# Layer 1's feed-forward output product: four of its eleven row blocks by seven half-size products, ordered by a build-time planner

## The chip, the cores and the metric

The kernel runs on one core of a Trainium2 chip. The metric is the device time of one execution in microseconds (us). The engines are PE (TensorE, the matrix multiplies; PEld is its weight load), DVE (VectorE), ACT (ScalarE), POOL (GpSimd) and SP (SyncE, which here only issues DMAs).

## The reference, cut to what matters

Two layers, each a mixer (a gated recurrence, then dilated attention) and a gated feed-forward part. There are 512 tokens, the model width is 1024, the inner width of the feed-forward part is 2816, and all is float32. The part that the change touches is the last product of layer 1:

```python
def swiglu_ffn(u, w_in, w_out):
    gate, up = jnp.split(u @ w_in, 2, axis=-1)
    return (jax.nn.silu(gate) * up) @ w_out        # (512 x 2816) @ (2816 x 1024)

y = swiglu_ffn(u, ffn_w_in[layer], ffn_w_out[layer])
h = h + (1.0 + g2) * rms_norm(y, norm_g[layer, 3])
```

`g2` is a row of 1024 numbers, the product of a conditioning vector with a 1024 x 1024 slice of `ada_w`, plus a bias.

## The kernel before

**How a float32 product is made.** Every operand is split into a high part, rounded to the fast float32 format by ACT (`act.copy`), and a low part, the rest, by DVE (`dve.tensor_sub`). A product is then three matmuls, high x high, high x low, low x high (`three`, L580). So each block of weights and each block of activations costs PE three passes, ACT one cast and DVE one subtraction. The views `SEEN`, `PLACED`, `SEEN2` and `PLACED2` (L38 to L41) bring every second element together, so a cast or a subtraction through them reads with a stride of two elements; `TAKE` and `LAID` do the same on PE's side.

**Weights.** `items` (L492 to L566) is the list of all loads in order, 1 MB each. `Stream` (L46) loads them through SP into two `raw` buffers; three pairs of `hi`/`lo` buffers hold split weights. Layer 1's list ends with 18 "quarters" items for the input product, then the 11 blocks of 256 rows of `w_out`, with the loads for `g2` (four "ada" items of 1 MB and two small "rows" items) woven in between.

**Layer 1's input product.** `seven_products` (L887) makes 18 column blocks by Strassen's scheme in Winograd's form: seven products of half size in place of eight. One pass per block: seven groups of twelve 256-column matmuls in the order `first`, `both`, `u2`, `first`, `u4`, `u2`, `u4`. ACT copies partial results from bank to bank between them (L993, L1002: `act.copy(s.u4, s.u2)`, on which the fifth group waits). The order on each engine is the order of the code (`manual_schedule`). At the end of a pass `gate_of` (L966, ACT) and `value_of` (L969, DVE) write one block of `mid`, the 2816 x 512 inner activations.

**Layer 1's output product** (`ffn`, L1060 to L1128). For j in 0 to 8: `st.take()` splits the weights of block j, two calls of `part` split two 128-row blocks of `mid`, and 48 matmuls of 512 columns (2 row blocks x 4 token blocks x 2 column halves x 3) add to eight PSUM banks, `y0` and `y1`. This loop lies in no hand-made order. The ada items are worked off inside `process_to` (L107): four DVE operations each (L397, L399), and per column half one all-reduce on POOL (L401) and two DVE operations on the gate (L446, L447). The last stage (L1107 to L1125) takes blocks 9 and 10 token block by token block, 24 matmuls each, then squares (L618), gates (L627), updates `h` and stores it.

**The planner** (`Plan`, L166; `planner`, L1471). The recurrence and the attention are laid out by it: each step is a task with an engine, a cost written by hand, the keys it reads and writes, and for PE a goal time. `run` computes due times backwards, tries 72 rules of a list schedule on those costs, and issues all tasks in the order of the best. `place` gives a ring of buffers; `load_next` issues the next load when a raw buffer comes free.

Of the kernel before, what the change touches and what calls it, by code (L numbers as in the profile page):

```python
# [17 lines left out]
P = 128  # L18
S = 512
# [298 lines left out]
def block_kernel(tc, x, c, positions, ada_w, ada_b, norm_g, hgrn_w_in, lower, hgrn_norm_g, hgrn_w_out,  # L318
# [8 lines left out]
    with ExitStack() as ctx:  # L327
# [237 lines left out]
        f1a, f1b = ffn_ws(1)  # L565
        items += f1a + weave(f1b[:9], ada_seq((1, 5)), 0) + f1b[9:]  # L566
        st = Stream(nc, wp, items, 2, 3)
# [318 lines left out]

        def seven_products(fs, mid, seeded, spare, th, tl):  # L887

# [80 lines left out]
            def value_of(i, s):  # L969
                dve.tensor_add(W[:, 3], W[:, 6 + i % 2], s.both)  # L970
                dve.tensor_add(W[:, 2], W[:, 4 + i % 2], s.u2)
                dve.scalar_tensor_tensor(H2(mid(fs[i])), W[:, 2:4], -1.0, W[:, 0:2], op0=OP.mult, op1=OP.mult)

            with tc.manual_schedule(engines=ORDERED):
# [10 lines left out]
                for i in range(len(fs)):  # L985
# [11 lines left out]
                    if before:  # L997
                        value_of(i - 1, before)
                    run(s.u2, Sm, 0, t2, False)
                    run(s.first, R, 1024, B21, False)  # L1000
                    act.copy(W[:, 4 + i % 2], s.both)
# [16 lines left out]
                gate_of(len(fs) - 1, before)  # L1018
                value_of(len(fs) - 1, before)

        def ffn(l, first, close, nxt, side):
            turns.close()
            close()
            with ExitStack() as fx:
# [4 lines left out]
                with ExitStack() as qx:  # L1029
# [6 lines left out]
                    for j in range(PLAIN[l]):  # L1036
# [14 lines left out]
                        if j == 0:  # L1051
                            cut()
                            fixed.close()
                    seven_products(range(2 * PLAIN[l], NF), mid, pss, spare, th, tl)
# [5 lines left out]
                y0 = [bank("mm") for _ in range(NT)]  # L1060
                y1 = [bank("a"), bank("b"), bank("a"), bank("b")]
                parts = {}

                def part(f):
                    oh, ol = fresh(roll, [P, S], "oh", 5, F32R), fresh(roll, [P, S], "ol", 5, F32R)
                    act.copy(PLACED(oh), SEEN(mid(f)))  # L1066
                    dve.tensor_sub(PLACED(ol), SEEN(mid(f)), PLACED(oh).bitcast(F32))
                    parts[f] = (oh, ol)
                NJ = NF // 2
                part(0)  # L1070
                part(1)

                def prods(t, f, w, k, halves=(0, 1)):
                    oh, ol = parts[f]
                    tok = slice(t * P, (t + 1) * P)
                    for n in halves:
                        a = slice(k * D + n * 512, k * D + (n + 1) * 512)
                        three((y0, y1)[n][t], oh[:, tok], ol[:, tok], w[0][:, a], w[1][:, a], f == 0, f == NF - 1)
                for j in range(NJ - 2):
                    if j == 2 and l == 0:  # L1080
                        with tc.tile_pool(name="angles", bufs=1, side=bass.opposite_side(side)) as rp:
                            rotary(rp)
                    w = st.take()
                    part(2 * j + 2)
                    part(2 * j + 3)
                    for k in range(2):
                        for t in range(NT):
                            prods(t, 2 * j + k, w, k)
                ws = [st.take(), st.take(1)]
                part(NF - 2)  # L1090
                part(NF - 1)
                mx.close()
                n = Turn(side, y0, y1, gates.pop((l, 5)), nxt and nxt[0])

# [375 lines left out]

        def planner(extra=(), end=0):  # L1471

# [26 lines left out]
            def load_next():  # L1499

                spot = seq[0] % (2 + len(extra))
                seq[0] += 1
                while st.items[to_load[0]][1] is None:
                    to_load[0] += 1
# [1012 lines left out]
```

## Time and profile before

| | |
|---|---|
| median of 3 runs | 1436.63 us (1436.47 to 1439.49) |
| profiled execution | 1437.54 us, its span 1435.7 us |
| PE busy, share of the span | 1406.7 us, 98% |
| DVE busy | 1119.5 us, 78% |
| ACT busy | 807.5 us, 56% |
| POOL busy | 204.9 us, 14% |
| mean granted TensorE clock | 0.997 of full speed |

The span runs from the first to the last instruction; what lies around it is 1.8 us. In the page a busy time is a sum over one engine's instructions, overlaps counted once; matmuls are pipelined, so a busy PE is one with no gap longer than its pipeline. Views by line give count, busy time, mean length of one in ns and the idle time before them with what ended it. The timeline gives start, length, engine, line, what is written and read, and the count of merged instructions.

### The profile page before, as it was taken

How to read it: one execution, taken by the hardware profiler on the slowest of the kernel's cores; microseconds unless marked ns; L12 is line 12 of the kernel's file. 1: busy time of each engine (PE TensorE's matmuls, PEld its weight loads, DVE VectorE, ACT ScalarE, POOL GpSimd, SP SyncE). 2: the span in 40 equal slices, each digit the busy share in tenths (PEclk: the TensorE clock that was granted, in tenths of full speed). 3: DMA queues.
4: the chain of work that ended last, by engine and by line, in shares of the span. 5: the costliest groups of instructions: out<-in, count | busy, mean ns of one | idle time of the engine just before them, and what ended most of it. 6: DMA issues, size and time to landing. Idle time of an engine off the chain costs nothing. (4 is left out here: it accounts for less than half of the span.)

```text
span 1435.7 us, 25151 instructions
## 1 busy us (share of the span) xinstructions
PE 1406.7 (98%) x9807; PEld 1304.7 (91%) x9807; DVE 1119.5 (78%) x1780; ACT 807.5 (56%) x1502; POOL 204.9 (14%) x179
## 2 busy tenths in 40 slices
PE   8999999999999999999999999999999999999998
PEld 6788899899999988888999999999988999999887
DVE  4589889587888898787888887888776978887644
ACT  4443434465655543376648888377876555555342
POOL 1023112130111112140001010001013111110100
PEclk9999999999999999999999999999999999999999
DMA  9655655132344377423254452444352434444541
GB/s 307 187 198 191 205 177 176 59 115 76 106 117 118 118 266 268 147 100 125 74 156 121 134 132 64 130 144 134 99 191 74 118 90 118 118 118 147 176 147 59
DMA packets 212871, 201.08 MB, mean 140 GB/s; under 512 B 8920, under 2 KB 170640, under 8 KB 212496
## 3 DMA queue, kind: packets, MB, share of 16 engines
q1 hardware_dynamic: 209776, 192.71, 43.0%
q10 hardware_dynamic: 1952, 6.65, 1.3%
q8 instruction: 77, 1.26, 0.4%
q0 software_dynamic: 1024, 0.12, 0.2%
q14 instruction: 42, 0.34, 0.1%
HBM read 192.30 MB, written 5.30 MB: 138 GB/s over the span
## 5 line engine op out<-in xcount | busy, mean ns | idle before, releaser
L1600 PE MATMUL ps_mm<-apart,hiq 128*128 128x256 f32 (+1 forms) x608 | 137.4, 320 | 1.6 <-ACT hiq L2113 0.8
L1600 PE MATMUL ps_mm<-uh,hiq 128*128 128x256 f32 (+1 forms) x416 | 134.6, 323 | 0.5 <-ACT ps_mm L2067 0.5
L1600 PE MATMUL ps_mm<-uh,loq 128*128 128x256 f32 (+1 forms) x416 | 131.2, 315 | 0.2 <-DVE loq L2025 0.2
L1600 PE MATMUL ps_mm<-ul,hiq 128*128 128x256 f32 (+1 forms) x416 | 131.0, 315 | 0.0
L1600 PEld LDWEIGHTS ps_mm<-apart,hiq 128*128 128x128 f32 x608 | 99.8, 191 | 7.7 <-ACT xs L2092 1.2
L954 DVE TENSOR_TENSOR loq<-raw,hiq 128x1024 fp32r<-128x1024 f32 x72 | 85.0, 1221 | 20.1 <-ACT hiq L950 20.1
L963 PE MATMUL ps_mm<-th,hiq 128*128 128x256 f32 x360 | 99.0, 275 | 0.0
L963 PE MATMUL ps_mm<-tl,hiq 128*128 128x256 f32 x360 | 99.0, 275 | 0.0
L963 PE MATMUL ps_mm<-th,loq 128*128 128x256 f32 x360 | 99.0, 275 | 0.0
L1600 PE MATMUL ps_mm<-apart,loq 128*128 128x256 f32 (+1 forms) x304 | 95.5, 314 | 0.7 <-DVE loq L2114 0.6
L934 POOL TENSOR_TENSOR raw<-raw 128x512 f32<-128x512 f32 x36 | 47.9, 1330 | 320.0 <-DVE spare L930 165.2
L1600 PEld LDWEIGHTS ps_mm<-uh,hiq 128*128 128x128 f32 x416 | 79.4, 191 | 5.1 <-ACT ps_mm L2067 0.9
L950 ACT CAST hiq<-raw 128x1024 fp32r<-128x1024 f32 x72 | 72.1, 1047 | 21.0 <-DVE raw L938 16.4
L1600 PEld LDWEIGHTS ps_mm<-uh,loq 128*128 128x128 f32 x416 | 79.4, 191 | 4.7 <-DVE loq L2025 0.4
L1600 PEld LDWEIGHTS ps_mm<-ul,hiq 128*128 128x128 f32 x416 | 79.4, 191 | 4.1 <-issue 0.5
L116 DVE TENSOR_TENSOR lo<-raw,hi 128x2048 fp32r<-128x2048 f32 x25 | 63.2, 2527 | 21.5 <-ACT hi L115 21.5
L1066 ACT CAST oh<-mid 128x512 fp32r<-128x512 f32 x44 | 37.4, 874 | 70.6 <-PE ps_b L583 61.9
L115 ACT CAST hi<-raw 128x2048 fp32r<-128x2048 f32 x25 | 47.6, 1905 | 43.0 <-DMA raw<-in_ffn_w_out_dram 31.6
L963 PEld LDWEIGHTS ps_mm<-th,loq 128*128 128x128 f32 x360 | 69.1, 192 | 0.0
L963 PEld LDWEIGHTS ps_mm<-tl,hiq 128*128 128x128 f32 x360 | 69.1, 192 | 0.0
L963 PEld LDWEIGHTS ps_mm<-th,hiq 128*128 128x128 f32 x360 | 69.1, 192 | 0.0
L582 PE MATMUL ps_mm<-hi,oh 128*128 128x512 f32 x176 | 66.9, 380 | 0.0
(475 smaller groups left out, 4800.7 us busy)
## 6 DMA issues: line engine op xcount, KB each, us to landing
raw<-in_ffn_w_in_dram SPq DMA_DIRECT2D x144, 256.0 KB, 4.0
raw<-in_ada_w_dram SPq DMA_DIRECT2D x32, 1024.0 KB, 6.2
raw<-in_ffn_w_out_dram SPq DMA_DIRECT2D x22, 1024.0 KB, 6.7
raw<-in_attn_w_in_dram SPq DMA_DIRECT2D x64, 256.0 KB, 4.4
raw<-in_attn_w_in_dram SPq DMA_DIRECT2D x12, 1024.0 KB, 5.2
raw<-in_hgrn_w_in_dram SPq DMA_DIRECT2D x11, 1024.0 KB, 5.4
third<-in_ada_w_dram SPq DMA_DIRECT2D x8, 1024.0 KB, 7.1
raw<-in_ffn_w_in_dram SPq DMA_DIRECT2D x8, 1024.0 KB, 6.3
```

Of the source, the lines that this page charges most:

```text
L115: self.nc.scalar.copy(hi, t)
L116: self.nc.vector.tensor_sub(lo, t, hi.bitcast(F32))
L582: pe.matmul(ps, ah, bh, start=start, stop=False, skip_group_check=part)
L934: pool.tensor_add(r[:, 2], r[:, 2], r[:, 0])
L950: act.copy(hi, src)
L954: dve.tensor_sub(lo, src, hi.bitcast(F32))
L963: pe.matmul(LAID(ps), w[x][:, a], TAKE(us[kt][y]), start=begin and kt + m == 0, stop=kt == 3 and m == 2, skip_group_check=True)
L1066: act.copy(PLACED(oh), SEEN(mid(f)))
L1600: pe.matmul(LAID(dst()), x, TAKE(y), start=begin and i == 0, stop=i == len(todo) - 1, skip_group_check=True)
```

## The change

Layer 1's output product is rebuilt. Its row blocks 0 to 3 (1024 of 2816 rows) are taken by seven products of half size, two token halves by two column halves by the even and odd 128-row blocks. Each product has 24 matmuls of 512 columns, in four steps j of six. For this their weights come as four "quarter" items (even or odd rows by column half, 1 MB each) in place of four row blocks. The sums of quarters are formed in place by DVE (`b_sub`), the sums of `mid` blocks too (`a_op`), and every sum is split again (`b_cut`, `a_cut`). Blocks 4 and 5 stay plain products, as pieces that the planner can put between; blocks 6 to 8 follow, and blocks 9 and 10 are split in the plan and multiplied in the old last stage. Seven more raw buffers are opened where `seven_products` had its scratch. All four engines' work of this stage, SP's loads included, is issued in the planner's order. The first product's operands are split earlier, in the last pass of `seven_products` (`OutStart`, called between its groups `u2` and `first`): one cast and one subtraction of 1024 strided elements and four of 512. Layer 0 is unchanged.

The products and plain pieces are named by the pairs of PSUM banks they add to (`F`, `U`, `E`, `Z`). The first seven-product step begins with `behind_first`, which also puts two matmuls into `U`.

```diff
-        items += f1a + weave(f1b[:9], ada_seq((1, 5)), 0) + f1b[9:]
+        SEVEN = 4
+        def quarter_items():
+            v = ffn_w_out[1].rearrange("(j k p) (n c) -> p k n j c", k=2, p=P, n=2)
+            return [("w", v[:, q // 2, q % 2, 0:4], None) for q in range(4)]
...
+        last_gate = ada_seq((1, 5))
+        items += f1a + quarter_items() + f1b[SEVEN:SEVEN + 2] + last_gate[0] + f1b[SEVEN + 2:SEVEN + 3] + last_gate[1] + last_gate[2]
+        items += f1b[SEVEN + 3:9] + last_gate[3] + last_gate[5] + f1b[9:]
...
                     run(s.u2, Sm, 0, t2, False)
+                    if sooner and not more:
+                        sooner()
                     run(s.first, R, 1024, B21, False)
...
+        class OutStart:
...
+            def __call__(self):
+                self.ring = st.part_tiles(0)
+                (hi, lo), src = self.a_place(0), groups_of(self.midt, 0, 0, 0)
+                act.copy(PLACED2(hi), SEEN2(src))
+                dve.tensor_sub(PLACED2(lo), SEEN2(src), PLACED2(hi).bitcast(F32))
+                for k in range(4):
+                    raw = st.raw[st.done][:, k * 512:k * 512 + 512]
+                    act.copy(uh[:, k], raw)
+                    dve.tensor_sub(ul[:, k], raw, uh[:, k].bitcast(F32))
...
+            extra = [roll.tile([P, 2048], F32, name=f"rawx{k}") for k in range(SEVEN)]
...
+            cost = lambda g, c: c * (0.08 + 0.23 * size(g))
+            def b_place():
+                def make():
+                    b_no[0] += 1
+                    k = (b_no[0] - 1) % 4
+                    return uh[:, k], ul[:, k]
+                return plan.place("B", 4, make)
...
+            def b_cut(j, q, ready=False):
+                b = b_place()
+                key = key_at(q, j)
+                if not ready:
+                    ACT(0.52, lambda: act.copy(b.t[0], at(q, j)[0]), [key], [b("h")])
+                    DVE(0.62, lambda: dve.tensor_sub(b.t[1], at(q, j)[0], b.t[0].bitcast(F32)), [key, b("h")], [b("l")])
+                return b
...
+            def b_sub(j, to, one, two):
+                DVE(0.61, lambda: dve.tensor_sub(at(to, j)[0], at(one, j)[0], at(two, j)[0]), [key_at(one, j), key_at(two, j)], [key_at(to, j)])
...
+            def a_cut(t, k, g, src=None, key=None, ready=False):
+                a = a_next()
+                if not ready:
+                    src = groups_of(midt, t, k, g) if src is None else src
+                    key = ("mid", 2 * t + k, g) if key is None else key
+                    ACT(cost(g, 1.0), lambda: act.copy(PLACED2(a.t[0]), SEEN2(src)), [key, ring()], [a("h")])
+                    DVE(cost(g, 1.15), lambda: dve.tensor_sub(PLACED2(a.t[1]), SEEN2(src), PLACED2(a.t[0]).bitcast(F32)), [key, a("h")], [a("l")])
+                return a
...
+            def a_op(g, f, to, one, two):
+                DVE(cost(g, 1.15), lambda: f(to[0], one[0], two[0]), [one[1], two[1]], [to[1]])
...
+            def product(dst, cut, q, begin, behind=None, ready=0):
+                for j in range(SEVEN):
+                    if j in (0, 4):
+                        a = cut(j // 4)
+                    b = b_cut(j, q, j < ready)
...
+                    PE(6 * 0.2159, go, [a("h"), a("l"), b("h"), b("l"), ring()], [d() for d in dst])
...
+            def behind_first(j):
+                b_sub(j, 0, 1, 0)
+                if j == 1:
+                    PE(0.43, lambda: [pe.matmul(U[t].t, uh[:, 0, 0:P], uh[:, 0], start=True, stop=True) for t in range(2)], [], [U[t]() for t in range(2)])
+            product(F, lambda g: a_cut(0, 0, g, ready=g == 0), 0, True, behind_first, 4)
+            for t in range(2):
+                ACT(0.5, lambda t=t: act.copy(U[t].t, F[t].t), [F[t]()], [U[t]()], urgent=True)
...
+            def first_sum(g):
+                a_op(g, dve.tensor_add, s1, a21, a22)
+                return a_cut(0, 0, g, *s1)
...
+            product(E, first_sum, 0, True, lambda j: b_sub(j, 0, 3, 0))
...
+            plain_splits(SEVEN)
+            plain_products(SEVEN, "FZ", True)
+            product(F, lambda g: a_cut(0, 1, g), 2, False)
+            plain_splits(SEVEN + 1)
+            plain_products(SEVEN + 1, "FZ")
+            product(U, second_sum, 0, False, lambda j: b_sub(j, 0, 2, 0))
+            for t in range(2):
+                DVE(0.61, lambda t=t: dve.tensor_add(E[t].t, U[t].t, held.t[:, t * 512:t * 512 + 512]), [U[t](), held(t)], [E[t]()], urgent=True)
+            product(Z, lambda g: a_cut(1, 1, g), 0, False, lambda j: b_sub(j, 1, 3, 1))
+            plain_products(SEVEN, "E")
+            product(E, fourth_sum, 3, False)
+            product(U, third_sum, 1, False)
+            plain_products(SEVEN + 1, "E")
...
+            for j in (SEVEN, SEVEN + 1):
+                plain_products(j, "U")
+            for j in range(SEVEN + 2, NF // 2):
+                plain_splits(j)
+                if j < NF // 2 - 2:
+                    plain_products(j)
...
+                n = 2 + len(extra)
+                spot = seq[0] if seq[0] < n else held + (seq[0] - n) % (n - held)
```

## Rows read from the trace of the kernel before

**Rows 1.** Page: span and busy time, share of the span and instructions, of each engine.

```profile
span 1435.7 us, 25151 instructions
PE 1406.7 (98%) x9807; PEld 1304.7 (91%) x9807; DVE 1119.5 (78%) x1780; ACT 807.5 (56%) x1502; POOL 204.9 (14%) x179
```

**Rows 2.** Busy time of each engine by stretch; columns in the first line.

```profile
core 0: us, PE busy (x) PEld busy (x) DVE busy (x) ACT busy (x) POOL busy (x), PEclk, DMA share, GB/s
1315.80:1408.50 92.70, 92.70 (x432) 81.16 (x431) 54.02 (x51) 35.44 (x31) 6.87 (x2) 1.00 0.44 148
```

**Rows 3.** ACT's timeline, last stage: the squares that follow each finished PSUM bank.

```profile
1419.33 0.60 ACT L618 ACTIVATE junk<-ps_b 128x512 bf16<-128x512 f32 x1
1424.51 0.60 ACT L618 ACTIVATE junk<-ps_a 128x512 bf16<-128x512 f32 x1
```

**Rows 4.** DVE by line and form, 1303 to 1412 us.

```profile
L116 DVE TENSOR_TENSOR lo<-raw,hi 128x2048 fp32r<-128x2048 f32 x11 | 27.0, 2453 | 12.8 <-ACT hi L115 12.8
L1067 DVE TENSOR_TENSOR ol<-mid,oh 128x512 fp32r<-128x512 f32 x22 | 18.1, 834 | 13.4 <-ACT oh L1066 13.4
L399 DVE SCALAR_TENSOR_TENSOR shared<-raw,cond,shared 128x512 f32<-128x512 f32 x14 | 10.5, 749 | 4.8 <-DMA raw<-in_ada_w_dram 4.6
```

**Rows 5.** ACT by line and form, same stretch.

```profile
L115 ACT CAST hi<-raw 128x2048 fp32r<-128x2048 f32 x11 | 21.0, 1907 | 29.5 <-DMA raw<-in_ffn_w_out_dram 27.8 <-PE ps_mm L963 1.8
L1066 ACT CAST oh<-mid 128x512 fp32r<-128x512 f32 x22 | 18.5, 868 | 26.0 <-PE ps_b L583 21.7 <-PE ps_mm L583 3.7 <-PE ps_mm L963 0.6
```

**Rows 6.** ACT and DVE by line and form in the planned attention stage, 650 to 1090 us.

```profile
L2049 ACT CAST hiq<-raw 128x1024 fp32r<-128x1024 f32 x32 | 33.5, 1046 | 9.0 <-DVE raw L2029 7.7 <-PE ps_mm L1600 0.9 <-DMA raw<-in_attn_w_in_dram 0.2
L2024 ACT CAST hiq<-raw 128x512 fp32r<-128x512 f32 x48 | 29.6, 616 | 21.6 <-DVE raw L2029 14.3 <-DMA raw<-in_attn_w_in_dram 6.9
...
L2029 DVE TENSOR_TENSOR raw<-raw 128x512 f32<-128x512 f32 x64 | 43.7, 688 | 4.4 <-DMA raw<-in_attn_w_in_dram 3.4
```

**Rows 7.** DVE's timeline, attention: a run of equal instructions (start, length, xcount).

```profile
694.94 4.62 DVE L2160 TENSOR_TENSOR loq<-raw,hiq 128x1024 fp32r<-128x1024 f32 x4
```

**Rows 8.** ACT's timeline, last pass of layer 1's input products.

```profile
1308.24 0.38 ACT L993 COPY ps_mm<-ps_b 128x256 f32<-128x256 f32 x1
```

**Rows 9.** Chain that ended last: the products of that pass (start, length, xcount).

```profile
1308.91 1.36 PE ps_mm L963 x12
1311.61 4.02 PE ps_mm L963 x36
```

**Rows 10.** ACT's and DVE's timeline: last silu, last mid block, runs of strided and plain work.

```profile
1319.79 0.41 ACT L967 ACTIVATE shared<-ps_mm 128x256 f32<-128x256 f32 x1
...
1316.68 2.33 DVE L1067 TENSOR_TENSOR ol<-mid,oh 128x512 fp32r<-128x512 f32 x3
...
1322.54 0.68 DVE L972 SCALAR_TENSOR_TENSOR mid<-shared 128x512 f32<-128x512 f32 x1
```

**Rows 11.** DVE and POOL side by side: one subtraction under an all-reduce.

```profile
1329.48 4.07 DVE L116 TENSOR_TENSOR lo<-raw,hi 128x2048 fp32r<-128x2048 f32 x1 [0.17 <-ACT hi L115]
...
1328.78 3.64 POOL L401 PARTITION_ALL_REDUCE shared<-shared  x1 [28.67 <-DVE shared L399]
```

**Rows 12.** Busy time by stretch in planned stages (columns as in rows 2).

```profile
690.00:710.00 20.00, 20.00 (x182) 20.00 (x181) 18.55 (x31) 11.04 (x18) 1.65 (x2) 1.00 0.35 113
910.00:930.00 20.00, 18.39 (x159) 17.75 (x158) 18.37 (x21) 8.70 (x9) 0.00 (x0) 1.00 0.33 98
...
650.00:1090.00 440.00, 431.67 (x3192) 408.17 (x3191) 349.58 (x756) 310.60 (x661) 35.64 (x38) 1.00 0.43 125
60.00:260.00 200.00, 197.85 (x1228) 175.87 (x1227) 175.92 (x288) 86.04 (x190) 40.90 (x32) 1.00 0.55 184
```

**Rows 13.** What PE waited for in the planned attention stage: us, times, longest.

```profile
PE ps_mm L1600 <- DVE loq L2160: 2.1, 4, 0.6
```

**Rows 14.** Page, DMA issues: the layers' output weights, KB each, us to landing.

```profile
raw<-in_ffn_w_out_dram SPq DMA_DIRECT2D x22, 1024.0 KB, 6.7
```

**Rows 15.** A stretch in which the granted clock fell (columns as in rows 2).

```profile
10.00:20.00 10.00, 6.93 (x43) 5.63 (x44) 7.12 (x17) 7.27 (x15) 2.89 (x4) 0.83 1.10 343
```

More of the change, by code (lines that the diff above doesn't have):

```diff
@@ L885, in token_sums, with seven_products @@
             return cut
-        def seven_products(fs, mid, seeded, spare, th, tl):
+        def seven_products(fs, mid, seeded, spare, th, tl, sooner=None):
             fs = list(fs)
@@ L1019, in seven_products, with groups_of, __init__, a_place @@
                 value_of(len(fs) - 1, before)
+        def groups_of(midt, t, k, g):
+            j = slice(0, min(4, SEVEN)) if g == 0 else slice(4, SEVEN)
+            return midt[:, 2 * j.start + k:2 * j.stop + k - 1:2, t * 256:t * 256 + 256]
+        class OutStart:
+            def __init__(self, midt):
+                self.midt = midt
+            def a_place(self, g):
+                return [t[:, g * 1024:g * 1024 + 1024].rearrange("p (s c) -> p s c", c=256) for t in self.ring]
+            def __call__(self):
[7 more added lines that the diff above has]
+                    dve.tensor_sub(ul[:, k], raw, uh[:, k].bitcast(F32))
@@ L1053, in ffn @@
                             fixed.close()
-                    seven_products(range(2 * PLAIN[l], NF), mid, pss, spare, th, tl)
+                    sooner = None if nxt else OutStart(midt)
+                    seven_products(range(2 * PLAIN[l], NF), mid, pss, spare, th, tl, sooner)
                 fl.drain()
@@ L1059, in ffn @@
                     st.fill()
-                y0 = [bank("mm") for _ in range(NT)]
-                y1 = [bank("a"), bank("b"), bank("a"), bank("b")]
+                NJ = NF // 2
                 parts = {}
[L1064 to L1071, printed above, removed]
                 def prods(t, f, w, k, halves=(0, 1)):
@@ L1077, in prods @@
                         a = slice(k * D + n * 512, k * D + (n + 1) * 512)
[L1078 to L1088, printed above, removed]
@@ L1089, in ffn, with part @@
-                ws = [st.take(), st.take(1)]
-                part(NF - 2)
-                part(NF - 1)
+                        three((y0, y1)[n][t], oh[:, tok], ol[:, tok], w[0][:, a], w[1][:, a], f == 0, f == NF - 1, nxt is None)
+                if nxt is None:
+                    y0, y1, ws = out_planned(midt, sooner, roll, parts)
+                else:
+                    y0 = [bank("mm") for _ in range(NT)]
+                    y1 = [bank("a"), bank("b"), bank("a"), bank("b")]
+                    def part(f):
+                        oh, ol = fresh(roll, [P, S], "oh", 5, F32R), fresh(roll, [P, S], "ol", 5, F32R)
+                        act.copy(PLACED(oh), SEEN(mid(f)))
+                        dve.tensor_sub(PLACED(ol), SEEN(mid(f)), PLACED(oh).bitcast(F32))
+                        parts[f] = (oh, ol)
+                    part(0)
+                    part(1)
+                    for j in range(NJ - 2):
+                        if j == 2 and l == 0:
+                            with tc.tile_pool(name="angles", bufs=1, side=bass.opposite_side(side)) as rp:
+                                rotary(rp)
+                        w = st.take()
+                        part(2 * j + 2)
+                        part(2 * j + 3)
+                        for k in range(2):
+                            for t in range(NT):
+                                prods(t, 2 * j + k, w, k)
+                    ws = [st.take(), st.take(1)]
+                    part(NF - 2)
+                    part(NF - 1)
@@ L1092, in ffn @@
                 mx.close()
-                n = Turn(side, y0, y1, gates.pop((l, 5)), nxt and nxt[0])
+                n = Turn(side, y0, y1, gates.pop((l, 5)) if nxt else gates.pop((l, 5)).t, nxt and nxt[0])
                 def mm(t, ks=range(4)):
@@ L1468, in block_kernel, with planner @@
         pre.close()
-        def planner(extra=(), end=0):
+        def planner(extra=(), end=0, held=0):
             plan = Plan()
@@ L1499, in load_next @@
             def load_next():
-                spot = seq[0] % (2 + len(extra))
+                n = 2 + len(extra)
+                spot = seq[0] if seq[0] < n else held + (seq[0] - n) % (n - held)
                 seq[0] += 1
+                if to_load[0] == len(st.items):
+                    return
                 while st.items[to_load[0]][1] is None:
```

91 lines of the change are left out of this document (added).

## The prediction

> **What bounds the kernel now.** I read the page first: PE is busy for 1406.7 of 1435.7 us, 98% of the span, DVE for 78% [rows 1]. So the time is PE's work plus the little that PE waits. Then the stage that is changed, by stretches: from 1315.8 to 1408.5 us PE is busy for all 92.7 us with 432 matmuls, at a granted clock of 1.00, while DVE is busy for 54.0 and ACT for 35.4 [rows 2]. That is nine blocks of 48 matmuls and no wait at all. A matmul removed here is therefore time gained in full, and a wait of PE that is new here is time lost in full; DVE has 38 us to spare on the whole, and the question is whether that spare lies where the change wants it.
>
> **Saved on PE.** In the last stage the second squares of two successive token blocks start at 1419.33 and 1424.51 [rows 3], 24 matmuls apart: 5.18 / 24 = 0.216 us for a matmul of 512 columns. Four plain blocks are 4 x 48 = 192 matmuls, seven half-size products 7 x 24 = 168. Minus 24 matmuls is -5.18 us; the two that open bank U are +0.43. **Sum -4.75 us.** What is planned is then 408 matmuls and those two, 88.5 us, where 93.3 stood.
>
> **The earlier start (OutStart).** It is put into the last input pass, on ACT between the copy to `u2` and the copy to `u4`, on which PE's fifth group waits. ACT begins it behind the copy of 1308.24 [rows 8]. That copy was held up by a cast of 2048 elements, which leaves this place; PE's first group ends at 1307.57 by the chain (1308.91 - 1.34 [rows 9]), so the copy of 0.38 is done at 1307.9. One strided cast of 1024: a plain 512 takes 616 ns and a plain 1024 takes 1046 [rows 6], a strided 512 takes 868 [rows 5]; so 1046 + 2 x (868 - 616) = 1550, some 1.5 in a row of casts. Four plain casts of 512 at 0.52 in a row (half of 1046) are 2.1. ACT is free at 1311.5, then come two copies, 0.28 and 0.36: `u4` is ready at 1312.1. PE wants it at 1311.6 by the chain [rows 9], at 1311.3 if a pipeline's length is taken off. **A wait of 0.6 us** (0.45 to 0.75) on a step that had none. DVE's part, one strided subtraction and four plain, ends by 1313.4 and is covered by PE's last two groups, which without it would wait for nothing.
>
> **The second product's start.** In the old code nobody waited for the last block of `mid`. Now DVE's order has `value_of` ahead of all planned work: it waits for PE's last group, ACT's silu (0.41) and its own 0.68 [rows 10], so DVE is free about 1.35 us after PE has begun the first product. Then a sum of 1024 (1.2), ACT's strided cast (1.5), DVE's strided subtraction (1.45), one plain low part (0.6) and three hand-overs of 0.15 (0.17 stands in [rows 11]): 6.5, or 7.1 if one more subtraction is put between. PE ends the first product and the two matmuls after 5.6. **A wait of 0.9 to 1.5 us.**
>
> **DVE's load in the seven products.** In a row, 1024 plain elements take 4.62 / 4 = 1.155 us [rows 7]; 512 plain 0.69 alone [rows 6] and about 0.61 in a row; 512 strided 2.33 / 3 = 0.77 [rows 10]; 1024 strided 1.155 + 2 x (0.834 - 0.69) = 1.44 [rows 4]. Up to the last step of the last product: 6 strided low parts of `mid` 8.6, 4 sums of them 4.6, 16 sums of quarters 9.8, 24 low parts of quarters 14.6, weights and `mid` parts of blocks 4 and 5 4.6 + 3.1, two adds 1.3. That is 46.6 us. DVE at its densest is busy for 18.55 and 18.37 of 20 us in the planned attention [rows 12], 92%: 46.6 / 0.92 + 1.35 = 52.0. PE needs the last step after six products and U's opening (31.5), the first halves of blocks 4 and 5 (10.4), one quarter of block 4 (2.6) and three steps (3.9): 48.4, or 51.0 if the planner brings the quarter of block 5 forward. So PE waits for 1.0 to 3.6 us in this half, the start of the second product among them. I take the middle of 1.0 and 3.6, and never less than the start: **2.4 us**. Rings of four B and two A places keep DVE from working further ahead.
>
> **The rest of the stage.** Blocks 6 to 10 need 5 x (2 x 1.155 + 2 x 0.77) = 19.3 us of DVE, the last adds 2.6, the gate 16 sums of 0.69 (0.749 alone [rows 4], less in a row) and four of 0.65, 13.6. DVE's whole is 82.1. One subtraction of 2048 took 4.07 us under POOL's all-reduce [rows 11], where the other ten took (27.0 - 4.07) / 10 = 2.29 [rows 4]; one such hit adds 1.8. 83.9 / 0.92 + 1.35 = 92.5, due some 3 us after PE's 88.5 (block 10's second half and the second gate are wanted 2.6 and 5.2 us into the last stage): 1.0 us of wait, less than the 2.4 that PE has waited by then, so it costs nothing more. ACT has under 50 us of work here and is covered. The planner's own costs count strided work as plain (1.15 and 0.62 for DVE, 1.0 and 0.52 for ACT), so its order comes true later than it reckons; that is in the above, which goes by rows.
>
> **Loads.** 1 MB lands in 6.7 us in the median [rows 14]. The two first quarters load during the input passes as blocks 0 and 1 did. The third can start once the scratch of the last but one pass is free, the next behind the sixth group of the last pass, 1.3 us ahead of the stage. At the 343 GB/s of [rows 15] 1 MB takes 3.1 us; at 3.6 each, overlapped, block 4 lands at 7 and block 5 at 11, ahead of their use at 16 and 21. Cost 0; one by one at 6.7 it would be 18.8 and 25.5, the bound that a rival takes.
>
> **Sum.** -4.75 + 0.6 + 2.4 = -1.75 us. Against the profiled execution, 1437.54 us (span 1435.7 and 1.8 around it), that is 1435.8; the median of the runs lies 0.9 lower, at 1436.63, so 1434.9.
>
> **A page against a row.** A strided cast of 512 takes 868 ns where a plain one takes 616 [rows 5, 6], and a strided subtraction 834 [rows 4] where a plain one takes 688 [rows 6].
> The Trainium skill, page SBUF — State Buffer, section Door 1, says that a compute engine may stride up to four float32 elements at full bandwidth, as long as accesses fall twice into a 16-byte line; a stride of two should then cost nothing. By it the load of the first half would fall to 44.3 and the sum would come to about -3.3. The rows here speak against it, and the sum stays with them.
>
> **Rivals.**
> *Waits absorbed.* The planner finds an order in which DVE runs ahead on the plain pieces of blocks 4 and 5, and PE waits only for OutStart and 0.5 more: -3.65, 1433.0 us. For it: from 690 to 710 us PE has no gap beside a DVE at 18.55 of 20 [rows 12], and the longest of PE's waits for a low part in attention is 0.6 [rows 13]. Against it: the late start of DVE by 1.35.
> *DVE becomes the bound.* Both all-reduces hit it (82.1 + 3.6 = 85.7) and it is busy for 88% only, as in the planned recurrence, 175.9 of 200 [rows 12]: 97.4 + 1.35 - 3 = 95.7 for PE's 88.5, a wait of 7.2: +3.05, 1439.7 us, **slower**. It decides where DVE's share in the stage falls below 85.7 / 94.3 = 91%. For it: attention's mean is 349.6 of 440, 79%, with PE waiting for 8.3. Against it: that DVE idled there for want of work too.
> *OutStart holds PE's reads.* It writes the first half of the tiles `uh` and `ul` while PE reads their second half. If those reads wait for the writes, the fourth group starts at 1313.4 and not at 1310.3: +2.5 more, 1437.4 us.
> *Loads one by one.* Block 4's weights are late by 3.6 in part beside the same wait: +2.5, 1437.4 us.
> *The clock.* From 10 to 20 us PE is busy for 6.9 of 10 and the granted clock is 0.83, between its levels of 1.2 and 2.4 GHz [rows 15]; in the planned stages, with PE's waits in them, it is 1.00 [rows 12]. If a product of 24 matmuls ran at the lower level: +5.2, 1440.1 us.
> The Trainium skill, page TensorE: Matmul & The Clock Gate, section What's actually happening, has an idle array lose half its pulses.
>
> **Chances.** Within 0.2% means 2.9 us either way, about what a measurement of this kernel tells from no change. Forecast 0.41 (its own range 1433.4 to 1436.2; 0.08 of it beyond the bound), waits absorbed 0.26, DVE the bound 0.17, held reads 0.08, late loads 0.06, clock 0.02. Faster 0.26 + 0.08 = 0.34; slower 0.17 + 0.02 = 0.19; same 0.47. The range goes from no wait at all, 1431.9, to the DVE-bound case, 1439.7, which leaves out the upper half of that case, the clock and little below.
>
> **What would show it.** In the changed profile the stage has 410 matmuls to the last stage; PE's waits list a low part or a sum (DVE) two or three times, together 1.5 to 3 us, most within 50 us of the stage's start; the copy to `u4` of the last pass starts at 0.6 us after its group could. Wrong would be: waits of PE in that list above 5 us or below 1, a wait for a DMA, a fourth group that waits for OutStart, or a clock below 1.00.

## The result: slower by 0.45%, and the profile after

The changed kernel takes 1444.79 us (median of nine runs, 1440.18 to 1448.25) beside 1438.15 us for the kernel before on the same chip. **The ratio is 1.0045, 95% interval [1.0028, 1.0063]: some 6.5 us slower.** The forecast was 1434.9 us, in a range that ended at 1439.7; the measured time lies beyond it. The kernel before came out 1.5 us higher too, at 1438.15 where the forecast started from 1436.63, so change stands against change: +6.6 for -1.75.

**Where the two traces part.** Up to the last input pass of layer 1 both kernels run the same work in the same order, but that pass begins anywhere from 1304 to 1315 us in the profiles of this study, without the change having a hand in it. Whole spans therefore say little about one profile. What follows compares the *last stretch*: from the first matmul of the last input pass to the end of the span. In the kernel before the pass starts at 1306.23 us by the chain, so the stretch is 1435.7 - 1306.23 = 129.47 us. In the changed kernel it starts at 1308.90: 1443.8 - 1308.90 = 134.90 us. **The change costs 5.4 us there**, which lies within the interval of the ratio (4.0 to 9.1 us).

The page of the changed kernel, answering to [rows 1]:

```profile
span 1443.8 us, 25203 instructions
PE 1406.6 (97%) x9785; PEld 1302.8 (90%) x9785; DVE 1148.2 (80%) x1836; ACT 823.6 (57%) x1538; POOL 207.1 (14%) x179
```

There are 22 matmuls fewer, 24 removed and two added, as planned. PE is yet no less busy, and 8 us more of the span are idle (1443.8 - 1406.6 = 37.2, where it was 29.0). The waits of PE in the last stretch (us in total, times, longest) say where:

```profile
PE ps_b L1178 <- ACT uh L1098: 4.4, 1, 4.4
PE ps_a L595 <- DVE loq L1152: 1.6, 2, 0.8
PE ps_a L594 <- ACT hiq L1151: 1.1, 1, 1.1
```

The same stretch by windows (columns as in [rows 2]):

```profile
1314.00:1324.00 10.00, 6.87 (x51) 6.36 (x49) 4.95 (x8) 3.23 (x8) 0.00 (x0) 1.00 0.33 107
1324.00:1331.00 7.00, 5.70 (x18) 4.69 (x19) 5.73 (x9) 4.47 (x8) 0.00 (x0) 0.76 1.05 408
...
1331.00:1391.00 60.00, 60.00 (x279) 52.54 (x278) 59.47 (x77) 37.64 (x49) 3.25 (x1) 1.00 0.28 93
```

PE loses time at both ends of the stage: the first two rows show the start, and the waits at L594 and L595 above lie in the last stage. In the 60 us of the third row it waits for nothing, though DVE is busy for 59.47 of 60 (in [rows 2] it was 54.0 of 92.7).

**The first loss: the two matmuls that open bank U.** They stand at L1178, in the middle of the first product. The chain in order of time (start, length, what):

```profile
1321.24 0.29 ACT shared L979
...
1321.56 0.70 DVE mid L984
...
1322.28 1.24 DVE shared L1119
...
1323.60 1.13 ACT hiq L1112
1324.72 0.53 ACT uh L1098
...
1325.30 0.73 PE ps_b L1178 x2
1326.03 4.28 PE ps_a L1131 x12
```

The two matmuls only have to open the bank; their operand is any tile, and the code takes `uh[:, 0]`, without naming it among the keys that the task reads. `uh[:, 0]` is the first of four B places. The plan, which knows of no reader, issues the cast for the second product's first step into that place (L1098) ahead of them. They then wait for that cast. On ACT it stands behind the cast of the second product's A operand (L1112), and this waits for the sum (L1119), the last block of `mid` (L984) and silu (L979). So the whole chain that the prediction reckoned for the *second* product's start has come to stand in the middle of the *first*: 4.43 us of wait. The 12 matmuls behind it take 4.28 us where 24 take 5.18, and the granted clock of that window is 0.76. Together (0.73 - 0.43) + (4.28 - 2.59) = 2.0 us more.

**The second loss: the last loads.** The end of the chain:

```profile
1399.00 5.11 DMA rawx<-in_ada_w_dram
...
1407.36 3.24 POOL shared L1776
...
1411.35 0.70 DVE gate L1806
1412.07 2.06 DMA rawx<-in_ffn_w_out_dram
...
1417.09 1.05 ACT hiq L1151
...
1418.17 1.24 DVE loq L1152
...
1419.45 0.48 PE ps_a L595
1419.93 0.22 PE ps_a L596
```

Each load starts where a DVE instruction has freed its buffer, down to the load of block 10, which waits for the last gate row to be read (L1806). The last stage's first token block has three matmuls that wait, 2.7 us in total, and loses 3.7 us with what the restarts cost (four of its matmuls take 0.48, one in a row 0.22).

One thing ahead of the prediction has to be put right here. It says that seven more raw buffers are opened. The code opens four (`range(SEVEN)`, with `SEVEN = 4`). Four of the six buffers hold the quarters for most of the stage, and only two are left to take turns.

**The sum.** 6.4 us at the opening, 3.7 at the end, less the 4.75 of saved matmuls: +5.4 us, the measured 134.90 - 129.47.

**What came as reckoned.** DVE's operations by line and form, as in [rows 4] and [rows 7]:

```profile
L1152 DVE TENSOR_TENSOR loq<-rawx,hiq 128x1024 fp32r<-128x1024 f32 x10 | 12.0, 1224 | 3.1 <-ACT hiq L1151 3.1
...
L1113 DVE TENSOR_TENSOR loq<-mid,hiq 128x1024 fp32r<-128x1024 f32 x4 | 6.2, 1559 | 0.2 <-ACT hiq L1112 0.2
L1113 DVE TENSOR_TENSOR loq<-shared,hiq 128x1024 fp32r<-128x1024 f32 x2 | 2.8, 1410 | 0.0
```

A strided subtraction of 1024 takes 1410 to 1559 ns (reckoned: 1.44 us) where a plain one takes 1224. The Trainium skill, page SBUF — State Buffer, section Door 1, has a stride of two float32 elements cost nothing; these rows, like [rows 4, 6], do not agree.

### The profile page after: what moved, and what is told of

The parts are those of the page before. It is cut to its first block, busy times and chain, and to the rows that moved or that the text cites. A ratio compares the mean times of both kernels' runs of the same rounds, so it can differ in the third digit from the quotient of the medians.

```text
span 1443.8 us, 25203 instructions
## 1 busy us (share of the span) xinstructions
PE 1406.6 (97%) x9785; PEld 1302.8 (90%) x9785; DVE 1148.2 (80%) x1836; ACT 823.6 (57%) x1538; POOL 207.1 (14%) x179
## 3 DMA queue, kind: packets, MB, share of 16 engines
q0 software_dynamic: 1024, 0.12, 0.2%
## 5 line engine op out<-in xcount | busy, mean ns | idle before, releaser
L975 PE MATMUL ps_mm<-th,hiq 128*128 128x256 f32 x360 | 99.0, 275 | 0.0
L975 PE MATMUL ps_mm<-tl,hiq 128*128 128x256 f32 x360 | 99.0, 275 | 0.0
L975 PE MATMUL ps_mm<-th,loq 128*128 128x256 f32 x360 | 99.0, 275 | 0.0
L946 POOL TENSOR_TENSOR raw<-raw 128x512 f32<-128x512 f32 x36 | 48.0, 1334 | 319.8 <-DVE spare L942 165.1
L975 PEld LDWEIGHTS ps_mm<-tl,hiq 128*128 128x128 f32 x360 | 69.1, 192 | 0.0
L975 PEld LDWEIGHTS ps_mm<-th,hiq 128*128 128x128 f32 x360 | 69.1, 192 | 0.0
L975 PEld LDWEIGHTS ps_mm<-th,loq 128*128 128x128 f32 x360 | 69.1, 192 | 0.0
L1826 PEld LDWEIGHTS ps_mm<-apart,loq 128*128 128x128 f32 x304 | 58.3, 192 | 4.7 <-DVE loq L2340 1.0
L595 PE MATMUL ps_mm<-ul,hi 128*128 128x256 f32 (+1 forms) x176 | 55.3, 314 | 1.6 <-DVE ul L694 1.6
L594 PE MATMUL ps_mm<-uh,hi 128*128 128x256 f32 (+1 forms) x176 | 55.4, 315 | 0.0
L596 PE MATMUL ps_mm<-uh,lo 128*128 128x256 f32 (+1 forms) x176 | 55.2, 314 | 0.0
```

What stands on the lines that cost most here:

```text
L594: pe.matmul(ps, ah, bh, start=start, stop=False, skip_group_check=part)
L595: pe.matmul(ps, ah, bl, start=False, stop=False, skip_group_check=part)
L596: pe.matmul(ps, al, bh, start=False, stop=stop, skip_group_check=part)
L946: pool.tensor_add(r[:, 2], r[:, 2], r[:, 0])
L975: pe.matmul(LAID(ps), w[x][:, a], TAKE(us[kt][y]), start=begin and kt + m == 0, stop=kt == 3 and m == 2, skip_group_check=True)
L1826: pe.matmul(LAID(dst()), x, TAKE(y), start=begin and i == 0, stop=i == len(todo) - 1, skip_group_check=True)
```

## The experiments

All stretches are taken as above, from one profile each; ratios are to the kernel before. The theory at the start was that of the two losses: **A**, each is a fault of its own (an operand that is rewritten, too few rotating buffers), worth what its wait lasts. The main rival, **B**, was that DVE is the bound, and that both waits are only where its lateness shows.

| run | ratio [95% interval] | last stretch, us |
|---|---|---|
| kernel before | | 129.47, again 129.73 |
| changed kernel | 1.0045 [1.0028, 1.0063] | 134.90 |
| e1, U opened from another tile | 1.0054 [1.0037, 1.0071] | 134.84 |
| e2, six more buffers | 1.0015 [1.0003, 1.0026] | 131.16 |
| e3, both | 1.0004 [0.9993, 1.0015] | 130.36 |
| e4, e3 in one written order | 0.9991 [0.9981, 1.0002] | 128.49 |
| e5, e4 with loads reckoned one by one | 1.0026 [1.0015, 1.0037] | 132.89 |
| e6, e5 with true prices | 1.0005 [0.9990, 1.0020] | 130.83 |
| e7, e6 with OutStart later | 1.0000 [0.9986, 1.0014] | 128.97 |
| e8, e4 with OutStart later | 0.9994 [0.9982, 1.0006] | 127.87 |
| e9, e8 with true prices | 0.9984 [0.9970, 0.9999] | 127.45 |
| e11, e9 once more | 0.9989 [0.9976, 1.0003] | 127.38 |
| e10, e9 with 20 low parts twice | one run | 140.28 |

**The kernel before, once more.**

> The kernel before, once more with a profile. In the profiles of the changed kernels the last input pass starts 1.7 to 6.3 us later than in the one of before, though all that stands ahead of it is the same program. Theory A (that is chance between executions, the attention's transfers above all): here it starts anywhere from 1306 to 1312 us, and the length from there to the end is 129.5 within 0.2. Theory B (the change slows what is ahead of it): it starts at 1306 to 1307 again.

The pass starts at 1307.07 us and the stretch is 129.73, for 129.47. The stretch repeats to 0.3 us, so smaller differences say nothing. The start at 1307.07 alone fits both theories. One kernel run as e9 and as e11 settles it: its pass starts at 1315.35 and at 1304.82 us.

**e1: open U from a tile that nobody rewrites.**

```diff
-PE(0.43, lambda: [pe.matmul(U[t].t, uh[:, 0, 0:P], uh[:, 0], ...) for t in range(2)], [], ...)
+PE(0.43, lambda: [pe.matmul(U[t].t.rearrange(...), begun.a_place(0)[0][:, 0, 0:P], begun.a_place(0)[0][:, 0:2], ...) for t in range(2)], [ring()], ...)
```

> The two matmuls that open bank U read the first product's A place, which is not rewritten before them, in place of uh[:,0], which the plan has rewritten by then. Theory A (PE stands still because these two wait for that later cast): the wait of 4.4 us at the opening is gone, the second half of the first product runs at once and at the full clock, and what is left is a wait of some 3 us for the second product's operands; time against the changed kernel -3 us (-2 to -4.5). Theory B (PE waits for DVE's load as a whole, the opening only shows where): the wait moves to the second product undiminished, -0.5 us or less.

The wait at the opening is gone, and the stretch is as long as before: 134.84. A's number missed. B's, at most 0.5 us, came true, though not by its reason: 2.7 us of the 4.4 moved to the second product. The waits of PE:

```profile
PE ps_a L595 <- DVE loq L1152: 2.2, 3, 0.8
PE ps_mm L1131 <- ACT uh L1098: 1.4, 1, 1.4
PE ps_mm L1131 <- DVE ul L1099: 1.3, 1, 1.3
PE ps_a L594 <- ACT hiq L1151: 1.3, 2, 1.0
```

At the start PE now waits 2.7 us for the second product's operands, and the clock falls all the same. What it gained there, it waits longer at the end. The chain shows when the last stage goes on:

```profile
1423.04 0.48 PE ps_a L595
```

Counted from the start of the pass (1312.56), the last low part reaches PE after 110.5 us; in the changed kernel it was 1419.45 - 1308.90 = 110.6. The end of the stage is timed by DVE, the buffers and the loads, not by PE, and a gain of PE ahead of it is lost there.

**e2: six more buffers, so that four take turns.**

```diff
-extra = [roll.tile([P, 2048], F32, name=f"rawx{k}") for k in range(SEVEN)]
+extra = [roll.tile([P, 2048], F32, name=f"rawx{k}") for k in range(SEVEN + 2)]
```

> Six extra raw buffers in place of four, so that four and not two take the loads from block 4 on in turn; nothing else. Theory A (the waits of 3.7 us at the start of the last stage come from blocks 9 and 10, whose loads stood behind buffers that the conditioning loads held): these waits are gone, -3.7 us (-3 to -4) against the changed kernel, the opening's wait unchanged at 4.4. Theory B (DVE is full for 60 us and would split these blocks late anyway): under 1 us of it goes.

The stretch is 131.16, 3.74 less, which is A's number. PE's list of waits holds one entry, the opening, 4.4 us as before. DVE has the same work as in the changed kernel, so B falls for the end of the stage: what was short there was buffers.

**e3: both.**

> Both edits together. Theory A: the sum of the two, -6.7 us against the changed kernel, which is -0.2 us or so against the kernel before. Theory B: DVE's full load sets the end of the stage, -2 us at most.

130.36 us, 4.5 less than the changed kernel, between A's 6.7 and B's 2: with the end out of the way the other edit counts, but for 0.8 and not for 3. PE's waits:

```profile
PE ps_mm L1131 <- ACT uh L1098: 2.3, 2, 1.4
PE ps_mm L1131 <- DVE ul L1099: 1.8, 2, 0.9
```

They are those of the second product's start, which the prediction had at 0.9 to 1.5. One reason is the order at the seam. The last input pass and the plan are two separately ordered parts, and the scheduler between them put 12 matmuls of the first product into the pass, where PE would have waited for OutStart. Seen in the changed kernel:

```profile
1316.47 0.38 PE L1131 MATMUL ps_a<-uh,loq 128*128 128x512 f32 x1
1316.69 0.27 PE L975 MATMUL ps_mm<-th,hiq 128*128 128x256 f32 x1
```

A matmul of the first product (L1131) stands there before the last groups of the pass (L975). OutStart's wait of 0.6 so went away, but half the first product was no longer there to cover the chain behind the last `mid` block, and the last groups of the pass came later.

**e4: pass and plan in one written order.**

```diff
-            with tc.manual_schedule(engines=ORDERED):
+            held_order = ExitStack()
+            held_order.enter_context(tc.manual_schedule(engines=ORDERED))
...
-            with tc.manual_schedule(engines=ORDERED | {mybir.EngineType.SP}):
-                plan.run()
+            plan.run()
+            begun.order.close()
```

> Both edits, and the order by hand of the input pass and the plan made one, so that the scheduler cannot put the first 12 matmuls of the first output product ahead of the last three groups of the input pass. Theory A (that early half takes away the cover that the second product's chain needs): PE waits 0.6 us in the input pass for the u4 copy, and some 1 us in place of 3 before the second product; -1.5 us against e3. Theory B (the place of the first product doesn't matter, the chain sets the second product): within 0.7 us of e3.

128.49 us, 1.9 less than e3. PE's waits:

```profile
PE ps_mm L1137 <- DVE ul L1105: 1.1, 2, 0.9
PE ps_mm L1137 <- ACT uh L1104: 0.8, 1, 0.8
PE ps_mm L975 <- ACT ps_mm L1022: 0.3, 1, 0.3
```

The last row is OutStart's wait, back where the prediction had it, at 0.3 for 0.6. This kernel is what the prediction had pictured: 128.49 - 129.47 = -1.0 us, for the forecast -1.75.

Where the 1.9 us come from stands in the two chains, e3 above and e4 below:

```profile
1319.56 9.39 DMA rawx<-in_ffn_w_out_dram
...
1331.94 1.35 PE ps_mm L1131 x5
```

```profile
1319.55 9.52 DMA rawx<-in_ffn_w_out_dram
...
1332.05 1.35 PE ps_mm L1137 x5
```

The load is that of block 4. It goes out when the sixth group of the pass has freed its buffer, and in e3 the 12 matmuls stand ahead of that group. Counted from the start of the pass, it lands at 21.0 us in e3 and at 19.2 in e4; the last low part of the second product, planned behind block 4's, lets PE go on at 24.00 and at 22.14. These 1.86 us are the whole difference. (The edit also takes SP out of the hand-made order; in both kernels the loads go out within 0.1 us of that group's end, so this did not move them.)

**e5: the plan reckons the loads one after the other; e6: true prices in the planner.** In e5 each load task of the plan waits for the one before. Such a task issues nothing, it only tells the plan when a load lands: on the chip the six loads at the start go out as in e4, 8.67 to 11.72 us after the start of the pass (8.68 to 11.75). In e6 the planner is also told the strided prices of the trace (ACT 1.5 and 0.78, DVE 1.45 and 0.77), and that DVE and ACT are busy for 1.35 and 0.55 us at the start.

```diff
 n_th = plan.add("DMA", 3.4, None, w=[p()], late=2.2)
+if held:
+    if landed:
+        plan.tasks[n_th]["deps"].add(landed.pop())
+    landed.append(n_th)
```

> e4, and in the plan alone each load is reckoned to begin after the one before it has been moved, as the queue does it; e4's plan reckoned block 4's weights as the first to land, though they are loaded third, and put ACT's cast of them ahead of the second product's last cast. Theory A (ACT stands in front of that load while PE wants the cast behind it): the waits of 1.7 us in the second product's last steps go, -1.5 us against e4. Theory B (DVE's chain of sums and low parts is what is late there): within 0.4 us of e4.

> e5, and the plan told what the rows show: strided casts 1.5 and 0.78 us, strided subtractions 1.45 and 0.77, DVE taken for the first 1.35 us and ACT for 0.55. Theory A (the order suffers from costs that are too low): -0.5 to -1 us against e5. Theory B (the work is the same and DVE is full for 60 us, so another order gives nothing): within 0.4 us.

e5 is 4.4 us longer than e4, which neither theory had. The second product's waits nearly go (0.2), as A reasoned, and a wait for block 4's split weights comes in their place: the plan, which now has the load late, puts their cast (L1157) behind other casts, and ACT begins it at 1328.20 us, some 4 us after the load has landed. Behind the wait the clock is half. PE's timeline:

```profile
1329.35 0.80 PE L594 MATMUL ps_a<-hiq,uh 128*128 128x512 f32 x1 [3.29 <-ACT hiq L1157]
1331.29 0.80 PE L595 MATMUL ps_a<-loq,uh 128*128 128x512 f32 x1 [1.15 <-DVE loq L1158]
1331.88 0.63 PE L596 MATMUL ps_a<-hiq,ul 128*128 128x512 f32 x1
1332.31 0.63 PE L594 MATMUL ps_a<-hiq,uh 128*128 128x512 f32 x1
```

In e6 the same wait is 0.4 + 1.6 us, and the stretch 130.83, 2.1 less than e5 for A's 0.5 to 1. What a plan believes of a load costs time either way: taken as too early (e4), the cast holds the second product; taken as too late (e5), PE waits for the cast.

**e7 and e8: OutStart behind the copy to `u4`.** The call moves from before group four to behind that copy, in e7 on top of e6, in e8 on top of e4.

```diff
-                    if sooner and not more:
-                        sooner()
...
                     act.copy(s.u4, s.u2)
+                    if sooner and not more:
+                        sooner()
```

> e6, with OutStart put behind ACT's copy to u4 instead of ahead of it. Theory A (PE's fifth group waits for OutStart's casts): the wait of 0.34 us there goes and nothing else comes, as the casts and low parts are done 0.3 us or more before the pass ends; -0.3 us against e6. Theory B (the first product then waits for its last low part): 0 to +0.6.

> The kernel of e4_one_order with OutStart moved behind the copy to u4 in the last input pass. Theory A (each of the faults costs what its wait lasts): the 0.34 us of PE's wait for the copy to u4 go and nothing else changes, since the first product's operands have two groups of the pass (5.3 us) to be split in; last stretch 128.49 - 0.34 = 128.15 us, ratio to the kernel before 0.9988. Rival B: OutStart now ends too late and the first product waits for it; the 0.34 us come back there and the stretch stays at 128.5, ratio 0.9991 or above.

e7's waits are e6's without the 0.3, yet it is 1.9 us shorter: in e6 the granted clock was 0.64 and 0.50 from 1334 to 1338 us, in e7 it is 1.00 throughout. With the same waits behind the start, all of that but the 0.3 may be chance, and the two ratios don't part the kernels. e8 gives 127.87, 0.62 less than e4 for A's 0.34: block 4's load lands 0.62 us earlier too (18.54 us after the start of the pass, for 19.16). What is left in e8 is 1.5 us of waits in the second product, 0.4 of them at its start. The chain shows what holds it later:

```profile
1315.27 9.50 DMA rawx<-in_ffn_w_out_dram
1324.79 1.05 ACT hiq L1157
1325.87 1.23 DVE loq L1158
1327.09 0.61 DVE ul L1105
1327.75 1.35 PE ps_mm L1137 x5
```

Block 4's weights, not wanted until later, take 9.50 us to land, third of six loads of 1 MB that go out within 4.5 us. Their cast and their low part (L1157, L1158) are planned ahead of one low part of the second product (L1105), and the engines keep their order: a late load holds work that doesn't need it.

**e9 and e11: e8 with the true prices, the loads reckoned free to overlap.**

> The kernel of e8_order_and_later with the planner told the strided prices that the trace shows (ACT 1.5 and 0.78, DVE 1.45 and 0.77) and DVE and ACT taken as busy for the first 1.35 and 0.55 us, and the loads left free to overlap, unlike e6_true_costs and e7_start_later. Theory A (what is left of the waits of the second product, 1.9 us, comes of an order reckoned with wrong prices): these waits fall to some 1.0 and the stretch to about 127.2 us, ratio 0.998. Rival B (what is left is the start itself: DVE must do 6.5 us of dependent work in 5.6 us of PE time, whatever the order, and the loads of the first three blocks share their bandwidth): waits of 1.5 to 3 us somewhere in the first 30 us, stretch 128 to 129.5, ratio 0.9985 to 1.000.

> The kernel of e9_true_costs_free_loads once more, since its ratio of 0.9984 has an interval that ends at 0.9999. Theory A (the last stretch is 2.0 us shorter than that of the kernel before, 127.45 for 129.47, and nothing else differs): ratio 0.9986 with an interval below 1. Rival B (the 0.9984 was the chance of the program ahead of the stretch, whose length varies by 7 us): ratio 0.9995 to 1.0005. The profile's stretch is again 127.3 to 127.6 us under both.

127.45 and 127.38 us, A's number; ratios 0.9984 [0.9970, 0.9999] and 0.9989 [0.9976, 1.0003]. PE's waits in e9:

```profile
PE ps_mm L1139 <- DVE ul L1107: 0.9, 2, 0.5
PE ps_mm L1139 <- ACT uh L1106: 0.7, 1, 0.7
```

They are 1.6, not A's 1.0, and e8's were 1.5 already: the true prices took nothing off them. As in e8 only the first, 0.5, is the start that B had in mind; the other 1.0 is block 4's load again, which lands at 1333.95 and holds the low part (L1107) that PE goes on with at 1336.94. (B's waits of 1.5 to 3 us so came, its stretch of 128 or more did not.) The gain over e8, 0.4 and 0.5 us, little more than the stretch repeats to, is in the middle: in e8 one product of 24 took 5.38 us and the piece behind it began with a matmul of 0.45, and in e9 the products of the chain take 5.18. By the stretch this version is 2.0 us faster than the kernel before in both profiles. By the ratio the first interval lies just below 1 and the second just reaches it, so the times alone do not yet show a gain.

**e10: how much spare has a full DVE?** In e9, the low part of each quarter from the third product on is written twice, 20 more subtractions.

```diff
-DVE(0.62, lambda: dve.tensor_sub(b.t[1], at(q, j)[0], b.t[0].bitcast(F32)), ...)
+DVE(0.62, lambda: [dve.tensor_sub(b.t[1], at(q, j)[0], b.t[0].bitcast(F32)) for _ in range(again)], ...)
```

> The kernel of e9_true_costs_free_loads with DVE's low part of each quarter written twice, the same value, in the third to the seventh product: 20 more subtractions of 512, 20 x 0.60 = 12.1 us more of DVE, in a stage where the trace shows DVE at 9.8 to 10.0 of 10 and PE waiting for nothing. Theory A (a full DVE stands at the edge: between the third product and the end of the planned work it idles for some 2 us, and the last gate sum is wanted some 7 us after it is made): waits of PE for low parts of 5 to 9 us, last stretch 132.5 to 136.5 us. Rival B (a busy share of 10 of 10 only says that DVE has work waiting and runs it early; the real spare is large): waits of under 2 us and a stretch below 129.5 us.

140.28 us: 12.8 more, for 12.1 us of added work, where A had 5 to 9. Both theories gave DVE some spare, and the time shows none. A window of e10, and then PE's waits:

```profile
1345.00:1355.00 10.00, 6.79 (x27) 4.42 (x26) 9.86 (x15) 2.50 (x5) 0.00 (x0) 1.00 0.00 0
```

```profile
PE ps_mm L1143 <- DVE ul L1111: 5.5, 8, 1.7
PE ps_b L1143 <- DVE ul L1111: 4.6, 7, 1.7
```

DVE's busy share (9.86 of 10) reads as it did without the added work (9.84 to 10.00 from 1345 to 1395 us in e9); only PE's waits tell that it has gone from just enough to too little. They grew by 9.1 us, from 1.6 to 10.7, so some 3 us of the work did find room; but there are 13 waits more, and at 0.26 us for a restart (0.48 for 0.22) these cost an estimated 3.4.

## Why the prediction was wrong

Two of the signs that the prediction named for being wrong came: waits of PE above 5 us (7.1) and a granted clock below 1.00 (0.76). The terms in turn:

**Right: the saving on PE.** "Minus 24 matmuls is -5.18 us" stands: the page counts 22 fewer with the two added, and a product of 24 takes 5.18 us in the chains of e4, e8 and e9.

**Wrong: "the two that open bank U are +0.43".** They were priced by their length alone. Their operand, and who writes it next, was not looked up. They cost 0.73 + 4.43 us, and half a product at the lower clock. e1 and e3 show that 4.43 is no sum to be won back by that edit: a chain of dependent work behind the last `mid` block is due there in any case, and without the opening the second product waits for it.

**Wrong: "Loads ... Cost 0".** Only the loads of blocks 4 and 5 were followed. The number of rotating buffers was read wrongly, and it was not asked when a buffer comes free at the end, with a full DVE in front of it. It cost 3.74 us by e2's profile. That buffers were short is shown by e2; that DVE freed them late because it put off the sums for `g2` is read from the chain and was not tried by itself. Block 4's load, too, was not free. It landed some 10 us into the stage (reckoned: 7) and well ahead of its use at 16, as the prediction said; but its cast and its low part were planned ahead of work for the second product, so by the engines' order its landing sets when that product ends, in e3, e4, e8, e9 and e11 alike. The prediction asked only whether a load comes ahead of its own use.

**Wrong in place: OutStart's 0.6.** It was right that ACT would be late for `u4` (0.34 in e4), but the seam between two ordered parts let the scheduler fill the wait with the first product. The prediction took the order on paper for the order on PE. e4 shows 1.9 us for the seam, all of them by way of block 4's load.

**Near in number, by luck: the second product's start, 0.9 to 1.5.** With the faults removed PE waits 1.9 us there in e4, 1.5 in e8 and 1.6 in e9. But the chain that the prediction added up, behind the last `mid` block, makes only 0.2, 0.4 and 0.5 of it; the rest is block 4's load. The 2.4 in all for DVE's load (the middle of 1.0 and 3.6 is 2.3) stands for those waits, and in the sixty microseconds behind the start nothing was lost. The margin was thinner than the 92% of [rows 12] made it, as DVE ran at 99% there and e10 found next to no spare.

**The rivals.** *The clock* had 0.02 and happened, not over a whole product but over part of a half: 12 matmuls took 4.28 us for 2.59, 1.7 lost where it had 5.2. *DVE becomes the bound* named the right engine and, with 1439.7, the side; but DVE's fullness showed, by the chain, through the buffers that it freed late, not through low parts that PE waited for; the 91% at which it was to decide (85.7 / 94.3) has no working in the prediction. *Held reads* did not come: in e4 the fourth group waits for nothing. *Loads one by one*: the first loads did land one after the other, but 2 to 3 us apart and not 6.7 (last section), so PE did not wait for block 4's own products; the loads of the last stage followed one another through two buffers, at the other end of the stage from where it was looked for.

**What the mechanism is worth.** With the opening, the buffers, the seam, OutStart's place and the planner's prices mended, the same seven products give 2.0 us by the stretch; the forecast was -1.75 for the change as it stood. That the two lie close is luck in part: about two thirds of the waits that are left come by a path that the forecast did not have.

## What to carry to other kernels

A dummy instruction has operands too: look up who writes them next, and declare the read, or a planner will put the writer ahead of it and a whole chain with it. An engine that is busy for 99% may cost nothing in the middle of a stage and much at its end, where the low-priority work that it put off frees the buffers of the last loads; so follow the last load of a stage as closely as the first. Where engines keep a planned order, a load delays whatever stands behind its cast, so tell the planner when loads really land (e4, e5). And a saving ahead of a point that another chain sets (e1: 110.5 and 110.6 us) is not measurable until that chain is shortened, so test such edits together as well as alone.

## What the runs showed of the hardware that was not expected

**The granted clock fell inside a stage whose pauses are short.** In the changed kernel it was 0.76 from 1324 to 1331 us, behind a pause of 4.43 us. In e1 it fell behind two pauses of 1.4 and 1.3 us with one matmul between:

```profile
1328.00:1330.00 2.00, 0.48 (x1) 0.19 (x1) 2.00 (x3) 2.00 (x4) 0.00 (x0) 1.00 1.05 394
1330.00:1332.00 2.00, 1.19 (x3) 1.01 (x4) 2.00 (x5) 1.18 (x3) 0.00 (x0) 0.61 1.04 407
1332.00:1334.00 2.00, 2.00 (x7) 1.60 (x6) 1.17 (x2) 0.39 (x1) 0.00 (x0) 0.54 1.04 414
```

In these stretches PE went on at the lower of the two levels (1.2 of 2.4 GHz): in the changed kernel its matmuls follow each other every 0.43 us, for 0.216, from 1326.4 to 1329.4 us, and in e1 the clock reads 1.00 again from 1334 to 1336 us. The Trainium skill, page TensorE: Matmul & The Clock Gate, section What's actually happening, has an idle array lose half its pulses, and these rows agree. But e3 has pauses of 1.42 and 0.89 and again 0.89 and 0.86 us and keeps 1.00, and e10 keeps it with PE busy for 6.79 of 10; and e6 and e7, with the same waits of 1.0, 0.4 and 1.6 us, read 0.50 and 1.00 behind them. So the waits alone do not tell, and where the edge lies these runs do not settle.

**Large loads that are issued together land one after the other.** In e8 the third and fourth quarters and blocks 4 and 5, 1 MB each, are issued from 1314.30 to 1315.8 us. They land 5.2, 7.5, 9.5 and 11.5 us after their own issue, at 1319.5, 1322.2, 1324.8 and 1327.3 us, some 2.6 us apart, while the DMA engines move some 400 GB/s in all (408 in the changed kernel's window from 1324 us). So the 9.50 us of block 4 are its place in the row. Late in the changed kernel's stage, with one load at a time, 5.00 and 5.11 us pass.
